# Loading a 480-column strip of one row group by sixteen DMAs of 15 to 1 and 8 partitions in a cross-entropy kernel

## Chip, cores, metric

The kernel runs on one core of a Trainium2 chip. The metric is the device time of one execution in microseconds (us). The kernel before takes 2431.3 us. Its runs lie between 2430.97 and 2431.59 us, so differences of half a microsecond can be read. All runs here are of the fast state, and the granted clock was 1.0 in each.

## The reference

Softmax cross-entropy over 8192 rows of 32000 float32 logits, 1.05 GB in all:

```python
logits_max = np.max(logits, axis=-1, keepdims=True)
log_sum_exp = np.log(np.sum(np.exp(logits - logits_max), axis=-1)) + logits_max.squeeze(-1)
log_probs = logits - log_sum_exp[..., np.newaxis]
loss = -log_probs[np.arange(batch)[:, None], np.arange(seq), labels]
```

## The kernel before

Partition `p` holds 64 consecutive rows; row group `g` is the g-th row of each partition. Each group is loaded in two halves of 128 x 16000 (8 MB). There are three buffers. ScalarE takes exp of each half in place, without subtracting the row's maximum, and sums it; GpSimd and VectorE pick out the label's logit and are nearly idle (busy 4% and 1% of the span). The first group and the last two are cut into smaller loads.

```python
plan(0, [[4000, 4000, 8000], [16000]], [(0, 0), (0, 1), (0, 2), (1, 0)])
for g in range(1, G - 2):
    plan(g, [[W], [W]], [(0, 0), (1, 0)])
plan(G - 2, [[W], [10000, 6000]], [(0, 0), (1, 0), (1, 1)])
plan(G - 1, [[7400, 5840, 2260], [4540, 3720, 2920, 1780, 1460, 1120], [960]], ...)
data = ctx.enter_context(tc.tile_pool(name="data", bufs=3))
# ... cut: label lists, gathers ...
for j, (g, b, at, n) in enumerate(loads):
    if b not in buffers:
        buffers[b] = data.tile([P, W], FP32, tag="t", name="t")
    t = buffers[b]
    c0 = col.get(g, 0)
    col[g] = c0 + n
    nc.sync.dma_start(out=t[:, at:at + n], in_=lg_pg[:, g, c0:c0 + n])
    # ... cut: picking the label's logit ...
    exp(g, t[:, at:at + n])          # ScalarE, accumulates the sum
    # ... cut: the logarithms and the subtraction near the end ...
```

A semaphore is a counter that a DMA raises as its parts land; in the trace each load raises one 16 times. The source does not show the semaphores. As built, the loads use eight DMA semaphores in turn, and a DMA is issued only after the DMA eight places earlier, which uses the same semaphore, has landed: in the trace of the kernel before, the last three loads are issued at 2387.04, 2395.85 and 2402.83 us, 0.01 to 0.06 us after the last landing eight places earlier. SP is the SyncE engine, whose queue issues all loads. In what follows a load's *place* is its number in SP's order, from 0; a *landing* is the moment at which one of the 16 DMA engines has finished its part of a load; a *packet* is what one engine moves at a time, here one partition's row of a load (128 packets of 64000 bytes in a full load). The last two full loads ahead of the change are places 124 and 125; the load that the change splits begins at place 126.

The softmax here doesn't subtract the row's maximum and nothing guards it: scores larger than these inputs give would overflow.

## Time and profile before

| | before |
|---|---|
| median time | 2431.30 us (4 runs) |
| span in the profile | 2429.5 us |
| HBM traffic | 432 GB/s mean, DMA engines busy throughout |
| ScalarE busy | 72% |
| one 128 x 16000 load | lands every 18.9 us, 41.6 us after its issue |

From the page of the kernel before: span; ScalarE's busy time and share; the DMA engines' busy tenths and GB/s in 40 slices; the chain that ended last; and the issues of the full loads (count, size, median us from issue to landing).

```profile
span 2429.5 us, 954 instructions
...
DVE 22.9 (1%) x63; ACT 1748.9 (72%) x281; POOL 86.6 (4%) x132
...
DMA  9999999999999999999999999999999999999998
GB/s 423 438 423 437 438 428 432 438 436 424 438 436 428 434 438 433 427 438 435 429 434 437 433 428 437 435 427 435 437 434 429 435 437 426 435 437 433 430 434 377
...
DMA 73%; ACT 24%; issue 2%; POOL 1%; SPq 0%; POOLq 0%; DVE 0%; ACTq 0%
...
t<-in_logits_dram SPq DMA_DIRECT2D x124, 8000.0 KB, 41.6
```

A load waits 41.6 us for 18.9 us of its own work, because two earlier loads are in the queue when it is issued: place 126 is issued at 2326.48 us, and places 124 and 125 land at 2330.26 and 2349.15 us. This is why the DMA row stays at 9 until the last slice: the engines always have work queued.

The waits of SP's queue in the kernel before (line, waited for: total us, times, longest us). The first line is SP waiting for ScalarE to free a buffer. The second is the turn of the eight semaphores: three late, small loads waited for an earlier load to land.

```profile
SPq L176 <- ACT t L168: 2326.2, 125, 26.5
SPq L176 <- DMA t<-in_logits_dram: 18.1, 3, 8.5
```

The timeline of the kernel before near the end (start us, us, engine, line, operation; in brackets the idle time before it and what ended it). The third exp is that of place 126, the load which the change splits.

```profile
2330.34 13.54 ACT L168 ACTIVATE t<-t 128x16000 f32<-128x16000 f32 x1 [3.89 <-DMA t<-in_logits_dram]
...
2349.23 13.54 ACT L168 ACTIVATE t<-t 128x16000 f32<-128x16000 f32 x1 [5.26 <-DMA t<-in_logits_dram]
...
2368.14 13.54 ACT L168 ACTIVATE t<-t 128x16000 f32<-128x16000 f32 x1 [5.28 <-DMA t<-in_logits_dram]
```

Three stretches of the kernel before (length; busy us of DVE, ACT, POOL; PE clock; DMA share; GB/s). A packet counts in the stretch in which it starts, so shares can pass 1.

```profile
2345.00:2350.00 5.00, 0.00 (x0) 0.77 (x1) 0.00 (x0) 1.00 0.95 410
2350.00:2355.00 5.00, 0.00 (x0) 5.00 (x1) 0.00 (x0) 1.00 0.95 410
2355.00:2360.00 5.00, 0.00 (x0) 5.00 (x1) 0.00 (x0) 1.00 1.01 435
```

The aim of the change is seen in the trace's semaphore updates: each load has 16, as many as the profile counts DMA engines, and they are read here as one per engine. These are the landings of two loads, in us after the first:

```
place 9 (lands from  154.37 us): 0 .14 .17 .19 .21 .26 .27 .31 .32 .35 .36 .36 .42 .43 .53 .65
place 138, the last (2422.78 us): 0 .24 .31 .32 .35 .40 .42 .44 .46 .49 .54 .66 1.17 1.91 1.93 2.55
```

Four engines fall behind during the run, one of them by 2.5 us, and the last exp waits for the slowest: it starts at 2425.41 us, after the landing at 2425.33. The trace also accounts for how they fall behind: at each of the seven instruction fetches during the run one engine steps back by 0.67 to 0.97 us, which is about the fetch's own packet (0.31 to 0.33 us) and the surplus of the slow 64000-byte packet beside it (0.35 to 0.65 us). This is read from the times and not tested.

### The profile page before, as it was taken

Reading aid. Unit: us, or ns where it says so; the run is one execution under the profiler, and the core shown is the slowest. Engines: PE = TensorE matmul, PEld = TensorE weight load, DVE = VectorE, ACT = ScalarE, POOL = GpSimd, SP = SyncE. Lnnn points to the kernel's source line nnn. Section 1 sums busy time; section 2 is a strip of 40 time slices with the busy share of each in tenths; the row PEclk is TensorE's granted clock in tenths of the full one; section 3 lists DMA queues with packets and bytes.
Section 4 is the critical chain, followed back from the end, with each engine's and each line's share of the span. In section 5 each row is a group of like instructions: output and inputs, shape, how many; then the busy total and the mean of one; then the engine's idle time right before and its main releaser. Section 6 shows DMA issues by size and latency. Waiting matters only on the chain.

```text
span 2429.5 us, 954 instructions
## 1 busy us (share of the span) xinstructions
DVE 22.9 (1%) x63; ACT 1748.9 (72%) x281; POOL 86.6 (4%) x132
## 2 busy tenths in 40 slices
DVE  0000000000000000000000000000000000000000
ACT  4777767777677767777677776777667776777769
POOL 0000000000000000000000000000000000000000
DMA  9999999999999999999999999999999999999998
GB/s 423 438 423 437 438 428 432 438 436 424 438 436 428 434 438 433 427 438 435 429 434 437 433 428 437 435 427 435 437 434 429 435 437 426 435 437 433 430 434 377
DMA packets 20583, 1048.74 MB, mean 432 GB/s; under 512 B 2656, under 2 KB 2784, under 8 KB 3296
## 3 DMA queue, kind: packets, MB, share of 16 engines
q1 hardware_dynamic: 20304, 1048.62, 99.8%
q10 hardware_dynamic: 144, 0.07, 0.0%
q14 instruction: 7, 0.06, 0.0%
q0 software_dynamic: 128, 0.00, 0.0%
HBM read 1048.64 MB, written 0.03 MB: 432 GB/s over the span
## 4 chain that ended last, share of the span: by engine, by line
DMA 73%; ACT 24%; issue 2%; POOL 1%; SPq 0%; POOLq 0%; DVE 0%; ACTq 0%
DMA t<-in_logits_dram 73%; ACT t L168 24%; POOL pk L182 1%; SPq L176 0%; POOLq L236 0%; ACT logsum_last L208 0%; DVE res_last L209 0%; ACT logsum L201 0%; POOLq L182 0%; ACTq L168 0%
## 5 line engine op out<-in xcount | busy, mean ns | idle before, releaser
L168 ACT ACTIVATE t<-t 128x16000 f32<-128x16000 f32 (+5 forms) x139 | 1734.8, 12481 | 676.7 <-POOL pk L182 635.7
L182 POOL INDIRECT_COPY pk<-t,lists 128x48 f32 x120 | 81.6, 680 | 2216.8 <-DMA t<-in_logits_dram 2216.8
L187 DVE COPY_PREDICATED own<-one_hot,pk 128x384 f32<-128x384 int32 x15 | 8.9, 593 | 2282.9 <-POOL pk L182 2282.9
L168 ACT ACTIVATION_READ_ACCUMULATOR t<-t 128x1 f32 x139 | 25.9, 186 | 0.0
L188 DVE TENSOR_REDUCE found<-own 128x8 f32<-128x384 f32 x15 | 8.3, 555 | 0.5
L114 POOL DMA_INDIRECT lab_logit<-in_logits_dram,idx x4 | 4.1, 1033 | 1.2 <-issue 0.9
L107 ACT ACT_TABLE_LOAD x1 | 1.3, 1283 | 1.2 <-PEq L225 1.2
L196 DVE TENSOR_REDUCE totals<-sums 128x63 f32<-128x315 f32 x1 | 0.5, 481 | 81.5 <-ACT t L168 81.5
L154 DVE TENSOR_SCALAR lists<-clamped,mine 128x64 uint16<-128x64 f32 x6 | 1.2, 364 | 0.0
L110 POOL TENSOR_TENSOR idx<-idx,labs 128x64 int32<-128x64 int32 x1 | 0.3, 318 | 7.5 <-DMA labs<-in_labels_dram 7.5
L202 DVE TENSOR_TENSOR res<-logsum,lab_logit 128x63 f32<-128x63 f32 x1 | 0.2, 225 | 24.9 <-ACT logsum L201 24.9
L157 DVE MEMSET own<- 128x384 f32 x1 | 0.4, 378 | 0.0
L140 DVE TENSOR_SCALAR one_hot<-entries,at_entry 128x48 int32<-128x48 f32 x1 | 0.3, 347 | 0.1
L129 DVE TENSOR_SCALAR mine_at<-mine 128x3 f32<-128x3 f32 x2 | 0.3, 170 | 0.1
L108 DVE MEMSET sums<- 128x315 f32 x1 | 0.3, 321 | 0.9 <-PEq L225 0.9
L132 DVE TENSOR_TENSOR mine<-mine,mine_at 128x3 f32<-128x3 f32 x2 | 0.3, 162 | 0.1
L208 ACT ACTIVATE logsum_last<-sums_last,part 128x1 f32<-128x1 f32 x1 | 0.3, 294 | 0.0
L125 DVE TENSOR_SCALAR mine<-part16f 128x1 f32<-128x1 f32 x3 | 0.3, 147 | 0.0
L135 DVE TENSOR_SCALAR mine_at<-mine 128x1 f32<-128x1 f32 x3 | 0.3, 147 | 0.0
L201 ACT ACTIVATE logsum<-totals 128x63 f32<-128x63 f32 x1 | 0.2, 238 | 0.0
L199 DVE COPY_PREDICATED lab_logit<-in_first,found 128x60 f32<-128x60 int32 x1 | 0.2, 231 | 0.0
L122 DVE TENSOR_SCALAR part<-part 128x1 int32<-128x1 int32 x1 | 0.2, 154 | 7.7 <-POOL part L111 7.7
(17 smaller groups left out, 2.7 us busy)
## 6 DMA issues: line engine op xcount, KB each, us to landing
t<-in_logits_dram SPq DMA_DIRECT2D x124, 8000.0 KB, 41.6
t<-in_logits_dram SPq DMA_DIRECT2D x1, 5000.0 KB, 35.9
t<-in_logits_dram SPq DMA_DIRECT2D x2, 2000.0 KB, 9.6
t<-in_logits_dram SPq DMA_DIRECT2D x1, 4000.0 KB, 21.3
t<-in_logits_dram SPq DMA_DIRECT2D x1, 3700.0 KB, 32.9
t<-in_logits_dram SPq DMA_DIRECT2D x1, 3000.0 KB, 42.7
t<-in_logits_dram SPq DMA_DIRECT2D x1, 2920.0 KB, 39.5
t<-in_logits_dram SPq DMA_DIRECT2D x1, 2270.0 KB, 26.4
```

What stands on the lines that cost most here:

```text
L107: nc.scalar.preload_act_table_set("natural_log_exp_and_others")
L108: nc.vector.memset(sums[:], 0.0)
L110: nc.gpsimd.tensor_tensor(out=idx[:], in0=idx[:], in1=labs32, op=ALU.add)
L114: nc.gpsimd.indirect_dma_start(out=lab_logit[:, g:g + 1], out_offset=None, in_=lg, in_offset=bass.IndirectOffsetOnAxis(ap=idx[:, g:g + 1], ...
L125: nc.vector.tensor_scalar(out=mine[:, q:q + 1], in0=part16f[:], scalar1=4.0 * q, scalar2=None, op0=ALU.add)
L154: nc.vector.tensor_scalar(out=lists[:, :, h, q], in0=clamped[:, h, :], scalar1=mine[:, q:q + 1], scalar2=None, op0=ALU.mult)
L157: nc.vector.memset(own[:], 0.0)
L168: nc.scalar.activation(out=ap, in_=ap, func=EXP, accum_out=s)
L182: nc.gpsimd.indirect_copy(out=pk[:, 2 * i + h, :], data=t[:], idxs=lists[:, g, h, 0:3], i_know_this_is_slow=True)
L187: nc.vector.copy_predicated(own[:], one_hot[:].unsqueeze(1).to_broadcast([P, NB * 2, NI]), pk[:])
L188: nc.vector.reduce_sum(out=found[:, :, g - NB + 1:g + 1].rearrange("p h g -> p g h"), in_=own[:].rearrange("p (g h) n -> p g h n", h=2), a ...
L196: nc.vector.reduce_sum(out=totals[:], in_=sums[:], axis=X)
```

## The change

The intent is to even this out. The strip of 480 columns of the last but one row group comes by DMAs on few engines (in the changed kernel one of 9 partitions has 9 landings, a load of all 128 has 16), "so that the first engines get more" and the last ones less.

```diff
+    STRIP = 480
...
-        nc.sync.dma_start(out=t[:, at:at + n], in_=lg_pg[:, g, c0:c0 + n])
+        if (g, c0) == (G - 2, 0):
+            p0 = 0
+            for k in list(range(15, 0, -1)) + [8]:
+                nc.sync.dma_start(out=t[p0:p0 + k, 0:STRIP], in_=lg_pg[p0:p0 + k, g, 0:STRIP])
+                p0 += k
+            assert p0 == P
+            nc.sync.dma_start(out=t[:, STRIP:n], in_=lg_pg[:, g, STRIP:n])
+        else:
+            nc.sync.dma_start(out=t[:, at:at + n], in_=lg_pg[:, g, c0:c0 + n])
```

The bytes stay the same. One DMA becomes 17.

## The prediction

> **What bounds it now.** The loads. The page shows the DMA engines 90% or more busy in every slice but the last, 432 GB/s mean, ScalarE 72%. A 64000-byte packet took 2.366 us; eight per engine make one 128x16000 load, and loads land every 18.9 us. A load is issued when ScalarE frees its buffer and lands 41.6 us later, so two older loads are always queued and the 16 engines never starve. The chain of waits is 73% loads, 24% ScalarE.
>
> The trace's 16 landings per load show the imbalance that the change aims at. Early loads land within 0.65 us from first to last engine; by the last load the spread is 2.55 us: twelve engines within 0.6 us, the others at +1.1, +1.9, +1.9 and +2.5 us. Seven instruction fetches of 8192 bytes (367, 723, 823, 1180, 1563, 1934, 1975 us) coincide with seven slow packets (2.7 to 3.0 us) and with most of these steps. The trace does not name engines, so I cannot see that the late ones are the last ones.
>
> **What the change does.** [...] At best it gains about 0.5 us. That is the intent.
>
> **What it costs.** The load DMAs use eight semaphores in turn, and each issue waits until the DMA eight places earlier has landed. Before shows this: the wait table has 3 waits of the queue for loads, 18.1 us; the last three load issues (2387.04, 2395.85, 2402.83) stand 0.01 to 0.06 us after the last landing eight places earlier. The built program of after has the same turn of waits.
>
> The 17 DMAs start at 2326.48 us (place 126). Places 126 to 131 go at once, 132 when 124 has landed (2330.26). Place 133, the eighth strip DMA, must wait for 125, the last full load in flight: 2349.15. Then nine more issues, at a pitch of 0.38 to 0.48 us as traced for back-to-back issues; estimated 0.45 each, so the 15520-column DMA starts at about 2353.2. Data starts 0.85 to 1.0 us after issue (traced at the start and the end), about 2354.2. The engines, done with 125 at 2346.6 to 2349.2, idle 5 to 7 us: a hole in a queue that never was empty. All of it is on the critical path.
>
> From there one engine has 76.15 us (first landings of 125 to the last load) minus 0.56 us of strip; plus about 0.4 us of cold start and the spread, now about 0.65 us because the pause lines the engines up again. Last landing about 2431.0 against 2425.33: +5.7 us. The ScalarE tail stays as it is.
>
> **Predicted: 2437.0 us, 2435.3 to 2439.6 (8 in 10). Faster by over 2%: 0.003; within 2%: 0.99; slower by over 2%: 0.007.**
>
> **Right if** the profile shows the strip's eighth issue at about 2349 us, the large DMA of that load at about 2353, DMA busy lower in the slice there, ScalarE's wait before that load's exp up from 5.3 to about 11 us, later landings spread under 1 us, and the tail moved as a block by 5 to 6 us.
>
> **Wrong if** the strip's issues do not wait for place 125 (then 2430.8 to 2431.5); if DMAs on fewer than 16 engines issue much slower (0.6 to 0.9 us each adds 2 to 4 us); or if a cold restart costs more than 0.4 us.

## The result, and the profile after

The changed kernel takes 2436.72 us (2436.62 to 2436.79, 4 runs) against 2431.30: ratio 1.0023, 95% interval 1.0008 to 1.0037. Ratios here are the mean time of one kernel's fast runs over that of the other's of the same rounds, so they are not quite the ratio of the medians that are quoted. The change costs 5.4 us, which is inside 2% but far outside the noise.

From the page of the changed kernel, the lines that answer to those above:

```profile
span 2434.9 us, 974 instructions
...
DVE 22.9 (1%) x63; ACT 1748.9 (72%) x281; POOL 87.3 (4%) x132
...
DMA  9999999999999999999999999999999999999999
GB/s 422 437 431 427 437 437 435 423 437 437 436 426 433 438 434 430 431 437 434 434 427 436 437 434 427 435 435 435 430 432 435 435 434 427 435 437 436 425 381 394
...
DMA 73%; ACT 24%; issue 1%; POOL 1%; SPq 0%; DVE 0%; POOLq 0%; ACTq 0%
```

The page hardly shows the loss. Its slices are 61 us long, so a pause of a few us leaves the busy digit at 9; only the GB/s of the last slice but one falls (381 against 434). The close views show it. First the waits of SP's queue in the changed kernel; the strip is L182, the ordinary loads are L187:

```profile
SPq L187 <- ACT t L169: 2277.7, 123, 26.4
SPq L187 <- DMA t<-in_logits_dram: 27.1, 4, 9.1
SPq L182 <- DMA t<-in_logits_dram: 20.6, 2, 19.2
SPq L182 <- ACT t L169: 18.5, 1, 18.5
```

The strip's DMAs now wait for loads to land, once for 19.2 us. The same three stretches in the changed kernel:

```profile
2345.00:2350.00 5.00, 0.00 (x0) 0.16 (x1) 0.00 (x0) 1.00 0.21 71
2350.00:2355.00 5.00, 0.00 (x0) 5.00 (x1) 0.00 (x0) 1.00 0.70 216
2355.00:2360.00 5.00, 0.00 (x0) 5.00 (x1) 0.00 (x0) 1.00 0.92 397
```

71 GB/s in place of 410: the engines have run dry. The chain that ended last in the changed kernel says why (start us, us, what):

```profile
2307.62 42.13 DMA t<-in_logits_dram
2349.76 0.02 issue
2349.77 0.27 SPq L182
2350.04 0.04 issue
2350.09 0.29 SPq L182
...
2352.34 0.27 SPq L182
2352.61 0.04 issue
2352.66 20.80 DMA t<-in_logits_dram
```

The chain goes from a load (place 125) to SP, through nine issues of the strip, to the large DMA (15520 columns), and on. SP's issuing is on the critical path here for 2.9 us. In the kernel before, the chain at this place goes from ScalarE straight to the load of place 126:

```profile
2312.82 13.64 ACT t L168 x2
2326.46 0.02 issue
2326.48 41.58 DMA t<-in_logits_dram
```

In that kernel SP's issuing is on the chain for 0.80 us at the very start and for 0.75 us near 2382 us, and not here. And the exps of the changed kernel:

```profile
2330.37 13.54 ACT L169 ACTIVATE t<-t 128x16000 f32<-128x16000 f32 x1 [3.86 <-DMA t<-in_logits_dram]
...
2349.84 13.54 ACT L169 ACTIVATE t<-t 128x16000 f32<-128x16000 f32 x1 [5.84 <-DMA t<-in_logits_dram]
...
2373.56 13.54 ACT L169 ACTIVATE t<-t 128x16000 f32<-128x16000 f32 x1 [10.10 <-DMA t<-in_logits_dram]
```

ScalarE waits 10.10 us for the split load in place of 5.28, and everything after it is 5.4 us late. The last load's landings end at 2430.76 us in place of 2425.33.

### The profile page after: what moved, and what is told of

Its sections match the earlier page's. It is cut to its first block, busy times and chain, and to the rows that moved or that the text cites. A ratio compares the mean times of both kernels' runs of the same rounds, so it can differ in the third digit from the quotient of the medians.

```text
span 2434.9 us, 974 instructions
## 1 busy us (share of the span) xinstructions
DVE 22.9 (1%) x63; ACT 1748.9 (72%) x281; POOL 87.3 (4%) x132
## 4 chain that ended last, share of the span: by engine, by line
DMA 73%; ACT 24%; issue 1%; POOL 1%; SPq 0%; DVE 0%; POOLq 0%; ACTq 0%
DMA t<-in_logits_dram 73%; ACT t L169 24%; POOL pk L193 1%; SPq L182 0%; SPq L187 0%; ACT logsum_last L219 0%; DVE res_last L220 0%; ACT logsum L212 0%; POOLq L193 0%; ACTq L169 0%
```

## The experiments

Four theories were tried. **W**: the eighth DMA of the split load waits for the last full load, the queue runs dry, and that is the cost. **S**: the cost is that bytes went to engines that were already late. **C**: every small DMA costs the engines a fixed 0.34 us (5.4 us over 16). **P**, which came up on the way: where rows are written sets how fast packets go, and the rows of a DMA on a few neighbouring partitions slow themselves and the large packets beside them. Eleven kernels ran, all with correct results. The diffs of 1 to 8 and of 11 are against the changed kernel, those of 9 and 10 against the kernel before; lines that only count rows or columns are left out. In the tables "before" of the same rounds has medians of 2431.17 or 2431.18 us.

### 1. The same number of DMAs, no skew: even16

```diff
-            for k in list(range(15, 0, -1)) + [8]:
-                nc.sync.dma_start(out=t[p0:p0 + k, 0:STRIP], ...)
+            for w in [30] * 16:
+                nc.sync.dma_start(out=t[:, a:a + w], in_=lg_pg[:, g, a:a + w])
```

> The 16 strip DMAs take 30 columns of all 128 partitions each, so every engine gets the same bytes; 17 DMAs as in the changed kernel. Theory W (the issue of the eighth DMA of that load waits until the last full load has landed, and the queue runs dry): the hole stays, 2436.2 to 2437.2 us. Rival S (the time went up because bytes moved to engines that were already late): the cost vanishes, about 2431.5 us. Rival C (each strip DMA costs the engines a fixed 0.34 us, 5.4 us over 16): about 2436.7 us, so this run does not tell W from C.

Measured: 2437.60 us, 0.4 us above the expected range and 0.9 us above the changed kernel. Each strip DMA is of all 128 partitions, as an ordinary load is (16 landings for 128 packets, and the 18.9 us from load to load are eight packets of 2.366 us), so it is taken to give every engine the same bytes. The cost stays, so S does not explain the 5.4 us. The excess is the pitch of the issues: a strip DMA of all 128 partitions is issued every 0.47 us here, one of 8 or fewer partitions every 0.32 us in the changed kernel, so the large DMA starts at 2353.43 us, not 2352.66.

### 2. and 3. One DMA below and above the turn of eight: even6 and even7

```diff
-            for k in list(range(15, 0, -1)) + [8]:
+            for w in [80] * 6:            # even6
+            for w in [60] * 6 + [120]:    # even7
```

> 6 strip DMAs of 80 columns of all partitions, then the large one, which is the seventh of that load and waits only for a load that landed at about 2330 us. W: no hole, 2431.3 to 2432.0 us (some 0.4 us for 48 more small packets an engine). C: 6 times 0.34 us, 2433.3 us.

> 7 strip DMAs of all partitions, so the large one is the eighth and waits for the last full load. W: a step against even6 although only one DMA is added: the large DMA is issued at about 2349.2 us in place of 2352.7, so 3.5 us less than the changed kernel, 2433.2 us (2432.7 to 2433.8). C: 0.34 us over even6.

Measured: even6 2431.63 us, even7 2433.36 us. Six small DMAs cost 0.46 us in all (C wanted 2433.3 us); the seventh alone costs 1.73 us. The timelines of even6 and then of even7 show the issues of the strip (L182), of the large DMA (L185), and the exp of the split load:

```profile
2326.38 2.70 SPq L182 DMA_DIRECT2D t<-in_logits_dram  x6
2330.15 0.33 SPq L185 DMA_DIRECT2D t<-in_logits_dram  x1
...
2368.46 13.54 ACT L169 ACTIVATE t<-t 128x16000 f32<-128x16000 f32 x1 [5.59 <-DMA t<-in_logits_dram]
```

```profile
2326.54 4.10 SPq L182 DMA_DIRECT2D t<-in_logits_dram  x7
...
2349.28 0.33 SPq L185 DMA_DIRECT2D t<-in_logits_dram  x1
...
2370.23 13.54 ACT L169 ACTIVATE t<-t 128x16000 f32<-128x16000 f32 x1 [7.25 <-DMA t<-in_logits_dram]
```

One more small DMA moves the large one from 2330 to 2349 us: from well before the last full load has landed to just after. From even7 to even16 the large DMA starts 4.15 us later, and the time rises by 4.24 us. W is shown; S and C are out as the main cost. Of the changed kernel's 5.4 us, even7, which has the wait and no issue after it but the large one, has about 2.2 us; the rest comes with the nine issues that follow the wait.

The wait is exact to 0.02 us in every kernel with more than six small DMAs:

| kernel | last landing of place 125 | issue at place 133 | large DMA issued | time |
|---|---|---|---|---|
| even7 | 2349.27 | 2349.28 | 2349.28 | 2433.36 |
| narrow | 2349.07 | 2349.08 | 2351.97 | 2436.62 |
| the change | 2349.76 | 2349.77 | 2352.66 | 2436.72 |
| reversed | 2349.74 | 2349.76 | 2353.07 | 2436.92 |
| even16 | 2349.24 | 2349.26 | 2353.43 | 2437.60 |

### 4. Another order, to find the late engines: reversed

```diff
-            for k in list(range(15, 0, -1)) + [8]:
+            for k in [8, 8, 7, 6, 5, 4, 3, 2, 1] + list(range(15, 8, -1)):
```

> The same 16 strip DMAs and sizes in another order: 8, 8, 7, 6, 5, 4, 3, then 2, 1, 15 to 9. W: the time stays at 2436.2 to 2437.3 us. Its use is in the landings of the first seven[...]. If the intent's picture is right (first engines early, last late), the late landings are absent from DMAs of 8 partitions and fewer. The trace of the changed kernel already has all four among DMAs of 9 partitions, so I expect at least three of them in DMAs of 8.

Measured: 2436.92 us, as expected. Its trace answers which engines are late. These are the landings of place 125 (last five, the first of them ordinary) and of the strip's DMAs with 8 to 3 partitions, us after 2300:

```
place 125    ... 47.54 48.11 48.34 48.43 49.74
8 partitions  47.36 47.39 47.39 47.55 | 48.46 48.70 48.80 50.11
7 partitions  47.56 47.56 47.75       | 48.63 48.88 48.99 50.28
6 partitions  47.74 47.76             | 48.80 49.06 49.18 50.45
5 partitions  47.91                   | 48.97 49.23 49.36 50.62
4 partitions  48.09                   | 49.15 49.42 50.81
3 partitions  48.28                   | 49.32 50.99
```

Each DMA of k partitions has k landings (and one early update), and each set is the one above without one. The changed kernel's DMA of one partition has one landing, at 2353.31 us. So the sets are read as nested, and an engine is numbered here by the smallest DMA that it serves: the first is in all of them, the fifth in those of 5 partitions and more. An early landing drops out when 8, 7 and 6 partitions are reduced by one; late ones drop out from 5 to 4 and from 4 to 3. So two late engines are the fourth and the fifth, the other two are among the first three, and **all four late engines are among the first five**. By this numbering the changed kernel gives the first engine 16 rows and the fifth 12, where all had 8 before. Its skew goes the wrong way.

### 5. and 6. The skew without the pause: skew5 and skew5_wide

```diff
-            for k in list(range(15, 0, -1)) + [8]:
+            for k in [45, 33, 21, 22, 7]:
-    STRIP = 480
+    STRIP = 1920        # skew5_wide only
```

> The strip of 480 columns is given to the engines as unevenly as in the change, but by 5 DMAs (45, 33, 21, 22 and 7 partitions[...]), so the large DMA is the sixth and waits for nothing new. W with the late engines among the first five: no hole, and the late engines get 4 rows of 71 ns more and some packet overhead: 2431.4 to 2431.9 us. If the late engines were the last ones: a little under the kernel before, about 2430.7 us.

> The same with a strip of 1920 columns, so 4 rows are 4 times 284 ns, 1.13 us. Late engines first: 2432.1 to 2432.8 us, about 0.85 us over skew5. Late engines last: about 1 us under the kernel before. If neither (engines beyond the lag do not matter): as skew5.

Measured: skew5 2432.83 us, skew5_wide 2438.03 us. The semaphores show the split: the five DMAs of skew5 have 15, 11, 7, 11 and 7 landings, so 3, 3, 3, 2 and 1 rows for each engine that they reach. With nested sets as in reversed, the first seven engines get 12 rows each, the next four 8, the next four 3 and the last none. The sign is the one expected for late engines first, the size is not: 1.65 and 6.85 us in place of some 0.5 and 1.3. So the skew itself costs time even without a pause, and something else comes with it. The packets point to it. A 7680-byte packet takes 0.59 us on average in skew5_wide (0.29 at least, 0.90 at most), and while the strip runs, 64000-byte packets of place 125 take up to 4.27 us, where all but a few take 2.37.

### 7. and 8. The reverse skew through GpSimd's queue: pool_high and pool_low

```diff
-            p0 = 0
-            for k in list(range(15, 0, -1)) + [8]: ...
+            for p0 in (112, 120):
+                for lo, hi in ((0, 1), (1, STRIP)):     # pool_low: ((1, STRIP), (0, 1))
+                    nc.gpsimd.dma_start(out=t[p0:p0 + 8, lo:hi], in_=lg_pg[p0:p0 + 8, g, lo:hi])
+            nc.sync.dma_start(out=t[0:112, 0:STRIP], in_=lg_pg[0:112, g, 0:STRIP])   # STRIP = 6800
```

The long DMAs of GpSimd's queue are meant to miss the late engines in pool_high and to hit them in pool_low. In which turn the engines serve this queue was assumed by the author.

> An attempt at the opposite skew: of a strip of 6800 columns, 112 partitions come by one DMA of the SP queue[...], the other 16 by two DMAs of 8 partitions from GpSimd's queue, each after a DMA of 8 partitions and one column. [...] Expected: 2430.0 to 2430.6 us, about 0.9 us under the kernel before, the last landings spread 1.6 us in place of 2.55. If the turn is otherwise: 2431 to 2433 us.

> As pool_high with long and short DMAs exchanged[...]: 2432.0 to 2432.6 us, 2 us over pool_high, last landings spread about 3.5 us or more. If the turn of GpSimd's DMAs is otherwise than assumed, pool_low is the lower one or they are equal.

Measured: 2448.07 and 2450.36 us. Both are far slower than the kernel before; the attempt failed. Only their difference, 2.3 us, agrees with the expected sign. Here too packets stretch: a 27200-byte packet, which at the rate of the 64000-byte ones (27.05 GB/s, 64000 bytes in 2.366 us) would take about 1.0 us, takes 1.97 us, and 64000-byte packets take up to 5.99 us. On which engines GpSimd's DMAs ran is not settled: the assumed turn is shown by no run here.

### 9. and 10. Does the destination slow the packets? probe_own and probe_crowded

In skew5_wide, with DMAs of 45 to 7 neighbouring partitions, 7680-byte packets took 0.59 us on average and 64000-byte ones up to 4.27 us. P puts this down to where the rows are written; by what means that would slow them no trace here shows. Both probes add the same four DMAs to the kernel before, and differ in the partitions of a scratch tile alone, every fourth one in probe_own and eight neighbours in probe_crowded:

```diff
+        if (g, c0) == (G - 2, 0):
+            for q in range(4):
+                nc.sync.dma_start(out=scratch[q:32:4, :], in_=lg_pg[8*q:8*q + 8, g, 0:1920])        # probe_own
+                nc.sync.dma_start(out=scratch[8*q:8*q + 8, :], in_=lg_pg[8*q:8*q + 8, g, 0:1920])   # probe_crowded
```

> The kernel before with 4 extra DMAs just ahead of the load that the change splits: each loads 8 rows of 1920 columns into a scratch tile, onto partitions q, q+4, ... q+28[...]. Theory P[...]: no contention, packets of 7680 bytes take about 0.29 us, the first eight engines are 4 times 0.29 us later, and as the last engine is among them the time is 2432.2 to 2432.6 us. Rival Q (DMAs on few engines, or small packets beside large ones, are slow in themselves): packets of 0.5 to 0.6 us as in skew5_wide, 2433.5 us or more.

> The same 4 extra DMAs, same sizes and engines, onto partitions 8q to 8q+7[...]. P: packets of 7680 bytes take about 1 us, large packets of the late engines are slowed as well, 2434.5 to 2437 us. Q: as probe_own.

Measured, packets from 2320 to 2375 us:

| | time | 7680-byte packets: mean (longest) | 64000-byte packets: longest |
|---|---|---|---|
| before | 2431.17 us | none | 2.37 us |
| probe_own | 2432.61 us | 0.292 us (0.298) | 2.38 us |
| probe_crowded | 2434.89 us | 0.437 us (0.685) | 3.86 us |

The timelines of probe_own, then probe_crowded, at the exp of place 125 and of the next load:

```profile
2349.18 13.54 ACT L169 ACTIVATE t<-t 128x16000 f32<-128x16000 f32 x1 [5.28 <-DMA t<-in_logits_dram]
...
2369.25 13.54 ACT L169 ACTIVATE t<-t 128x16000 f32<-128x16000 f32 x1 [6.44 <-DMA t<-in_logits_dram]
```

```profile
2351.06 13.54 ACT L169 ACTIVATE t<-t 128x16000 f32<-128x16000 f32 x1 [6.96 <-DMA t<-in_logits_dram]
...
2371.53 13.54 ACT L169 ACTIVATE t<-t 128x16000 f32<-128x16000 f32 x1 [6.84 <-DMA t<-in_logits_dram]
```

Same bytes, same number of rows, same turn: only the destination partitions differ, and one set slows itself and the large packets beside it. That the destination slows packets is shown, in the sign that P expects; by what means is not shown. My size for it was wrong: I expected about 1 us for a crowded packet, an estimate without a measured source, and it was 0.44, likely because the engines reach these packets spread over 2.5 us and not all at once (not tested). probe_own's 1.44 us is a little over four packets (1.17 us): the first eight engines are on the critical path, as experiment 4 has it.

### 11. The change with next to no bytes in the strip: narrow

```diff
-    STRIP = 480
+    STRIP = 16
```

> The change with a strip of 16 columns: the same 17 DMAs in the same turn, but 64-byte rows, so next to no bytes move between engines. W: the hole stays. The large DMA brings 1856 bytes a row more, 0.55 us. If the slip of the last full load in the changed kernel (2349.76 against 2349.15 us) came from strip rows[...] (P), it goes back to about 2349.2 us and the eighth DMA is issued then; 2436.4 to 2437.0 us in all. If moved bytes were the cause (S), about 2431.3 us.

Measured: 2436.62 us. Moving no bytes gives the same time, so the amount moved is not the cost. The slip of place 125 is gone (last landing 2349.07 us, longest 64000-byte packet 2.38 us against 2.83 in the changed kernel), as P has it; what that saves, the large DMA takes back with its wider rows (1856 bytes more a row and 8 rows an engine, an estimate of 0.55 us at 27.05 GB/s).

No variant beat the kernel before. Nothing that was learned points to one on this path: the late engines are among those that the small DMAs of SP's queue load: in reversed a DMA of 5 partitions has all four late landings, and one of 3 still has two.

## Why the prediction was right

The predicted time was 2437.0 us and the measured one 2436.72. Point by point:

- **The wait at the eighth strip DMA** was right, and experiments 2 and 3 show it by adding one DMA. It was foreseen for 2349.15 us; it came at 2349.77, because place 125 itself landed 0.6 us later. That slip was not in the prediction. It goes with where the rows of small DMAs are written: narrow, with next to no bytes in those rows (last landing 2349.07 us), and probe_own, with rows on every fourth partition (exp of place 125 at 2349.18 us), do not have it; probe_crowded, with rows on eight neighbours, does (2351.06 us).
- **The nine issues** were over-sized: 0.45 us each was taken from DMAs of 128 partitions. Small ones took 0.32 us, so 2.9 us in place of 4.05.
- **Issue to first data**: 0.85 to 1.0 us foreseen; 0.97 measured (2352.66 to 2353.63).
- **The cold start** was under-sized: 0.4 us foreseen. The eight 62080-byte packets of an engine took 2.398 us on average after the pause; the median is 2.293, so 0.84 us in all. In even6, which has no pause, the mean is 2.303. Nearly all of it is in the first packet of each engine, 3.12 us on average (16 packets). In even16, which has the pause and moves no rows between engines, that first packet took 2.98 us, so most of the 0.84 us comes with the pause and not with the skew. The prediction gives no source for its 0.4 us, the author's estimate; the trace of the kernel before had a cold start to read, at its own beginning, where the first packet of each engine took 1.20 us on average against a median of 0.60. A restart of over 0.4 us is one of the prediction's own "wrong if" signs, and it came true; the total stayed near the forecast because the issues cost less than foreseen.
- **Spread of later landings**: 0.65 foreseen, 0.55 measured.
- **ScalarE's wait** before that load: about 11 us foreseen, 10.10 measured. The tail moved as a block.
- **A sign that failed**: I looked for a lower DMA busy digit in the slice. It stays at 9; only its GB/s falls.
- **The intent's gain** of at most 0.5 us was not judged in the prediction, which could not see which engines are late. The 0.5 us was an estimate: 8 rows of 1920 bytes fewer on the last engine, 71 ns each (64000 bytes take 2.366 us), make 0.57 us. The gain is negative: skew5, a similar skew without the pause, took 1.65 us more than the kernel before. All four late engines are among the first five, and packets are slowed (64000 bytes take up to 2.83 us in the changed kernel in place of 2.37).

The sum: 0.61 (slip) + 2.90 (nine issues) + 0.97 (first data) + 0.84 (cold start) + 0.55 (new spread) - 0.57 (strip already loaded, an estimate from 8 rows of 1920 bytes at 27 GB/s) = 5.3 us, against 5.43 us between the last landings of the two kernels. The predicted sum was close partly by luck: terms sized too high (the issues, by 1.2 us) and too low (the slip by 0.6, the cold start by 0.4) cancel. Its terms as written add up to 2430.84 us and not to "about 2431.0".

Two things stay open: why these four engines and no others take the steps (all seven steps stand at an instruction fetch, but the trace names no engine), and which part of the 17 us of pool_high is the 112-partition DMA and which GpSimd's own.

## What to carry to other kernels

Count DMAs, not only bytes, where loads share a small set of semaphores: a split load is cheap as long as its pieces fit in the turn that is open, and costs a drained queue from the first piece that does not; here six pieces cost 0.46 us and the seventh 1.73 us more. Before evening out engines, find from nested small DMAs which ones are late, and check by the packets that the place where the moved rows are written does not slow them and those beside them (here 0.437 us for 7680 bytes in place of 0.292, and up to 3.86 us for 64000 bytes in place of 2.37). A pause of 5 us does not show in a busy digit of a 61 us slice; look at the issuing queue's waits and at stretches of a few us.
